# Turning the w_up blocks of a hybrid decoder layer: transposing DMA transfers of 16-bit halves in place of PE transposes

## The chip, the cores and the metric

The kernel runs on one core of one Trainium2 chip. Such a core has five engines that run side by side, each in the order of its own instruction list: TensorE (PE in the profile; it multiplies matrices and, with an identity matrix as operand, transposes), VectorE (DVE), ScalarE (ACT), GpSimd (POOL) and SyncE (SP), whose only work here is to issue DMA transfers. Sixteen DMA engines carry out the transfers of all of them. SBUF is the large on-chip memory of 128 partitions, PSUM the small one that PE writes its results to. The metric is the time of one execution in microseconds (us) on the device.

## The reference, cut to what matters

One decoder layer is computed for 256 tokens of width 2048: a mixer (a state-space half and an attention half between two projections), and then a feed-forward part of width 8192 with a squared ReLU. The change touches the feed-forward part alone:

```python
D_MODEL = 2048; SEQ = 256; DEPTH = 1; D_FF = 4 * D_MODEL

def squared_relu_mlp(u, w_up, w_down):
    hdn = jax.nn.relu(jnp.einsum('bsd,df->bsf', u, w_up))
    return jnp.einsum('bsf,fd->bsd', hdn * hdn, w_down)

def reference(...):
    ...
    h = h + rmsnorm(mix, norm_mix_post[i])
    ff = squared_relu_mlp(rmsnorm(h, norm_mlp_pre[i]), w_up[i], w_down[i])
    h = h + rmsnorm(ff, norm_mlp_post[i])
```

Everything is float32.

## The kernel before, in words

**Products in three parts.** A float32 product is made of three faster ones. Each operand x is split into a rounded part (hi, of type float32r) and the rest (lo). `split` (line 145) does it: ScalarE copies x into hi (line 147), VectorE subtracts hi from x (line 148). PE then adds hi*hi, hi*lo and lo*hi in PSUM.

**Weights.** A tile of weights is 256 rows by 512 columns, 512 KB, held as 128 partitions x 1024. SP loads it into a raw slot (line 161, `fetch`), ScalarE and VectorE split it into one of five pairs of tiles called hi and lo, and PE multiplies it with the activations. A raw slot is free again when VectorE has made lo of it, a hi/lo pair when PE has used it. `RAWS = 4` raw slots always exist; each stage adds some in buffers that lie idle (`room["raw"]`).

**Units.** The work of the projections is done in units of two column blocks (2 x 512) and 256 tokens (two token tiles t of 128), with the 2048 rows of w_up in 8 steps k. A step is done either plainly (`row_tiles`: two weight tiles, 12 matmuls each) or, for a pair of column blocks together, by a scheme of seven products in place of eight (`seven`: two loaded tiles a and b, a sum e and a half tile t4 made from them by VectorE, 21 matmuls in all). For w_up the steps 1, 3, 4 and 6 are done by `seven`. After the last of them `combine_new` puts sums of the extra accumulators into four tiles of 128x512, `room["shared"]` (made of the buffers hb and wpost), and step 7 ends the unit. The seven products need sums of the activations too (`sums_of_acts`), kept in `room["sums"]`.

**Order.** The two halves of w_up and w_down (4096 columns and rows each) are done in turn: w_up half 0 (first block otherwise, then three units), w_down half 0 (two units), w_up half 1 (four units), w_down half 1 (two units). Weight loads and splits are pushed ahead of other work (`AHEAD`); the framework's scheduler lays down the order of each engine's list, and each engine follows it in order.

**Turning.** The result of a w_up unit, 128 tokens x 512 features for each of two blocks and two token tiles, is relu'd and squared and must then be turned, features to partitions, to serve as the activations of w_down. At the end of a block `up_end` makes r on VectorE (line 1450), ScalarE applies ReLU and Square (lines 1451, 1452), and `turned` lets PE do four transposes of 128x128 (line 1463) into the PSUM bank that the block has left; `split` then writes the parts into the activation tiles (sh/sl, ah0/al0, ah1/al1). A queue `waiting` with `pump` spreads this over the following steps. There are 12 results to turn in half 0 and 16 in half 1.

**Buffers.** In half 0 the four extra raw slots of the w_up units lie in mw0, mw1 and mw2; in half 1 three extra slots lie in a buffer ha. When w_down half 0 begins, `beside_down` makes a new ha, which holds the first sums of the activations. When w_down half 1 begins, a new ha gives three of its extra raw slots, uc two others.

Of the kernel before, what the change touches and what calls it, by code (L numbers as in the profile page):

```python
# [10 lines left out]
F32 = mybir.dt.float32  # L11
F32R = mybir.dt.float32r
BF16 = mybir.dt.bfloat16
AF = mybir.ActivationFunctionType
ALU = mybir.AluOpType
# [62 lines left out]
def hymba_layer(ctx: ExitStack, tc: tile.TileContext, x, norm_mix_pre, w_in, conv_w, conv_b, dt_bias, a_log,  # L78
# [113 lines left out]
    def beside_up(raws, turn):  # L192

        room["sums"] = [v[:, k:k + KB] for k in range(0, NK // 2, KB) for v in att[1]]
        b = hp.tile([P, NT, NB], F32, name="hb")
        room["shared"] = [[b[:, t] for t in range(NT)],
                          [hp.tile([P, NB], F32, name="wpost", bufs=2) for _ in range(NT)]]
        room["raw"], room["turn"], room["acts"], room["chain"] = raws, turn, act_u, True
        sums_of.clear()
# [124 lines left out]

    def row_tile(dst, t, parts, k0, acts, begin, end, cs=slice(0, NB)):
# [9 lines left out]
    def row_tiles(src, c0, ks, acc, acts, first=True, last=True, lag=0, at_end=None, pumps=1, fetch=fetch, halves=None):  # L335
# [4 lines left out]
        for i in range(n + lag):  # L340
# [14 lines left out]
            pump(pumps)  # L355

# [94 lines left out]
    def unit(src, n, order, last, acc, more, combine, lag=0, at_end=(None, None), first=True, ending=None,  # L451
# [5 lines left out]
        for i, (k, by_seven) in enumerate(order):  # L457
            if i + 1 < len(order) and order[i + 1][1]:
                sums_of_acts(order[i + 1][0])
            if by_seven:  # L460
# [4 lines left out]
                seven(src, *cols, k, acc, more, k == sevens[0], k == sevens[-1])  # L465
            else:
# [3 lines left out]
            if k == sevens[-1]:  # L470
                combine(more)
# [973 lines left out]
    def up_end(fb, b):  # L1445

        def at_end(t, acc):
            with tc.high_priority(offset=AHEAD):
                r = tmp() if t else hp.tile([P, NB], F32, name="junk")
                nc.vector.tensor_tensor(r, acc, room["shared"][b][t], op=ALU.subtract if b else ALU.add)  # L1450
                nc.scalar.activation(r, r, AF.Relu, scale=rmlp[:, t:t + 1])
                nc.scalar.activation(r, r, AF.Square)
            waiting.append(turned(t, 4 * fb, r, acc, 1 - b))
        return at_end

    def turned(t, k, r, p, later):
        for _ in range(later):
            yield
        ts = slice(t * P, (t + 1) * P)
        with tc.high_priority(offset=AHEAD):  # L1460
            with tc.issue_after(product[0].ins), tc.issue_after(product[1].ins):
                for f in range(4):
                    nc.tensor.transpose(p[:, f * P:(f + 1) * P], r[:, f * P:(f + 1) * P], ident)  # L1463
            d_h, d_l, i = part(k)
            split(d_h[:, i:i + 4, ts], d_l[:, i:i + 4, ts], p.rearrange("p (f s) -> p f s", f=4))
# [17 lines left out]
    for hf in range(2):  # L1483
        if hf:
            a = hp.tile([P, 3 * KB, NB], F32, name="ha")
            beside_up([*(a[:, k:k + KB] for k in range(0, 3 * KB, KB))], 0)
        for fb in range(0 if hf else 2, 8, 2):
            unit(w_ups[hf], fb, orders[("up", hf), fb], (7,), acc, more,
                 lambda x: combine_new(room["shared"], x), 0, (up_end(fb, 0), up_end(fb + 1, 1)))
            acc, more = more, acc  # L1490
        if hf == 0:
# [65 lines left out]
```

## Time and profile before

| what | value |
|---|---|
| runs timed | 1453.19, 1455.0, 1452.5 us; median 1453.19 us |
| span of the profiled execution, first to last instruction | 1451.4 us |
| median of the runs less that span | 1.8 us |
| packets of DMA, bytes, mean rate | 172359, 332.97 MB, 229 GB/s |
| time of the two w_down stages and the w_up stages together | about 790 to 1437 us of the span |

The profile is of one execution. Busy time counts the stretches in which an engine had an instruction under way; instructions of one engine overlap at their ends, so that the time from start to start is less than the duration of one. A "chain" follows the work that ended last back to the start; a "releaser" is what ended an engine's idle time.

### The profile page before, as it was taken

Reading aid. Unit: us, or ns where it says so; the run is one execution under the profiler, and the core shown is the slowest. Engines: PE = TensorE matmul, PEld = TensorE weight load, DVE = VectorE, ACT = ScalarE, POOL = GpSimd, SP = SyncE. Lnnn points to the kernel's source line nnn. Section 1 sums busy time; section 2 is a strip of 40 time slices with the busy share of each in tenths; the row PEclk is TensorE's granted clock in tenths of the full one; section 3 lists DMA queues with packets and bytes.
Section 4 is the critical chain, followed back from the end, with each engine's and each line's share of the span. In section 5 each row is a group of like instructions: output and inputs, shape, how many; then the busy total and the mean of one; then the engine's idle time right before and its main releaser. Section 6 shows DMA issues by size and latency. Waiting matters only on the chain.

```text
span 1451.4 us, 20394 instructions
## 1 busy us (share of the span) xinstructions
PE 1442.4 (99%) x7042; PEld 1214.7 (84%) x7042; DVE 1300.4 (90%) x1881; ACT 947.1 (65%) x1351; POOL 162.3 (11%) x244
## 2 busy tenths in 40 slices
PE   9999999999999999999999999999999999999998
PEld 8888888888888888888888888888888888888886
DVE  7788888988999788689988999999889999999998
ACT  7577669665666666556657677656465776766664
POOL 0201110131111000010100011010111110101000
PEclk9999999999999999999999999999999999999999
DMA  8977656756898658588976798688888888788854
GB/s 267 272 219 222 189 175 187 239 170 195 231 253 248 196 127 244 173 270 257 280 225 217 210 311 240 203 221 251 249 255 279 255 245 247 210 293 265 248 179 160
DMA packets 172359, 332.97 MB, mean 229 GB/s; under 512 B 16048, under 2 KB 18976, under 8 KB 172256
## 3 DMA queue, kind: packets, MB, share of 16 engines
q1 hardware_dynamic: 144736, 272.37, 58.1%
q0 software_dynamic: 19648, 45.63, 15.7%
q10 hardware_dynamic: 7872, 13.68, 2.8%
q8 instruction: 55, 0.90, 0.3%
q14 instruction: 48, 0.39, 0.1%
HBM read 327.39 MB, written 49.84 MB: 260 GB/s over the span
## 4 chain that ended last, share of the span: by engine, by line
PE 76%; ACT 1%; DVE 1%; DMA 0%; issue 0%; ACTq 0%
PE acc L331 10%; PE acc L333 10%; PE acc L332 10%; PE acc L418 7%; PE acc L419 7%; PE acc L420 7%; PE acc L485 4%; PE ps L331 3%; PE ps L332 3%; PE ps L333 3%; PE ps L418 2%; PE ps L419 2%; PE ps L420 2%; PE acc L488 2%; PE acc L1463 1%; PE ps L938 0%
## 5 line engine op out<-in xcount | busy, mean ns | idle before, releaser
L148 DVE TENSOR_TENSOR lo<-raw,hi 128x1024 fp32r<-128x1024 f32 (+1 forms) x387 | 470.1, 1220 | 79.1 <-ACT hi L147 76.3
L147 ACT ACTIVATE hi<-raw 128x1024 fp32r<-128x1024 f32 (+1 forms) x387 | 404.2, 1050 | 204.2 <-PE acc L333 71.4
L485 PE MATMUL acc<-ua,hi 128*128 128x512 f32 x520 | 141.2, 401 | 0.1
L147 ACT ACTIVATE hi<-e 128x1024 fp32r<-128x1024 f32 x66 | 70.2, 1063 | 68.5 <-DVE e L252 62.7
L485 PEld LDWEIGHTS acc<-ua,hi 128*128 128x128 f32 x520 | 91.3, 189 | 14.2 <-ACT hi L147 0.2
L331 PE MATMUL acc<-hi,ua 128*128 128x512 f32 x228 | 90.6, 397 | 0.0
L332 PE MATMUL acc<-lo,ua 128*128 128x512 f32 x228 | 89.3, 392 | 0.0
L333 PE MATMUL acc<-hi,ua 128*128 128x512 f32 x228 | 89.2, 391 | 0.0
L331 PE MATMUL acc<-hi,sh 128*128 128x512 f32 x220 | 86.9, 395 | 0.0
L333 PE MATMUL acc<-hi,sl 128*128 128x512 f32 x220 | 85.8, 390 | 0.0
L332 PE MATMUL acc<-lo,sh 128*128 128x512 f32 x220 | 85.7, 390 | 0.0
L488 PEld LDWEIGHTS acc<-ua,lo 128*128 128x128 f32 x520 | 76.5, 190 | 8.9
L148 DVE TENSOR_TENSOR lo<-e,hi 128x1024 fp32r<-128x1024 f32 x66 | 80.5, 1220 | 0.0
L488 PE MATMUL acc<-ua,lo 128*128 128x256 f32 x520 | 78.8, 282 | 0.0
L419 PE MATMUL acc<-lo,ah 128*128 128x512 f32 x180 | 70.1, 390 | 0.0
L420 PE MATMUL acc<-hi,al 128*128 128x512 f32 x180 | 70.1, 390 | 0.0
L418 PE MATMUL acc<-hi,ah 128*128 128x512 f32 x180 | 70.1, 390 | 0.0
L485 PE MATMUL acc<-uc,hi 128*128 128x512 f32 x208 | 61.4, 405 | 0.0
L148 DVE TENSOR_TENSOR lo<-ha,hi 128x1024 fp32r<-128x1024 f32 x43 | 52.5, 1221 | 6.0 <-ACT hi L147 5.8
L147 ACT ACTIVATE hi<-ha 128x1024 fp32r<-128x1024 f32 x43 | 45.2, 1057 | 19.4 <-PE acc L333 12.4
L147 ACT ACTIVATE hi<-r 128x512 fp32r<-128x512 f32 x66 | 41.5, 629 | 20.8 <-PE acc L333 8.8
L418 PE MATMUL acc<-hi,ua 128*128 128x512 f32 x137 | 53.7, 392 | 0.0
(572 smaller groups left out, 3722.3 us busy)
## 6 DMA issues: line engine op xcount, KB each, us to landing
raw<-in_w_in_dram SPq DMA_DIRECT2D x154, 512.0 KB, 4.5
raw<-in_w_down_dram SPq DMA_DIRECT2D x69, 512.0 KB, 5.7
raw<-in_w_up_dram SPq DMA_DIRECT2D x65, 512.0 KB, 4.8
raw<-in_w_out_dram SPq DMA_DIRECT2D x38, 512.0 KB, 5.1
raw<-pair SPq DMA_DIRECT2D x57, 256.0 KB, 4.3
pair<-in_w_up_dram POOLq DMA_DIRECT2D x56, 256.0 KB, 5.4
pair<-in_w_down_dram POOLq DMA_DIRECT2D x52, 256.0 KB, 6.3
pair<-in_w_in_dram POOLq DMA_DIRECT2D x42, 256.0 KB, 5.5
```

The lines of the kernel that those rows point to most:

```text
L147: return (nc.scalar.activation(hi, src, AF.Copy), nc.vector.tensor_tensor(lo, src, hi.bitcast(F32), op=ALU.subtract))
L148: nc.vector.tensor_tensor(lo, src, hi.bitcast(F32), op=ALU.subtract))
L331: nc.tensor.matmul(dst[:, cs], a_h[:, r, ts], hi[:, j, cs], start=begin and j == 0, stop=False)
L332: nc.tensor.matmul(dst[:, cs], a_h[:, r, ts], lo[:, j, cs], start=False, stop=False)
L333: product[t] = nc.tensor.matmul(dst[:, cs], a_l[:, r, ts], hi[:, j, cs], start=False, stop=end and j == KB - 1)
L418: nc.tensor.matmul(dst, a_h, hi[:, j], start=own and first, stop=False)
L419: nc.tensor.matmul(dst, a_h, lo[:, j], start=False, stop=False)
L420: nc.tensor.matmul(dst, a_l, hi[:, j], start=False, stop=own and last)
L485: nc.tensor.matmul(acc[f], hi[:, j, f * P:(f + 1) * P], u(k0 + j), start=k0 + j == 0, stop=False, skip_group_check=True)
L488: nc.tensor.matmul(acc[f][:, 0], lo[:, j, f * P:(f + 1) * P], u(k0 + j)[:, 0], start=False, stop=k0 + j == NK - 1, skip_group_check=True)
L1463: nc.tensor.transpose(p[:, f * P:(f + 1) * P], r[:, f * P:(f + 1) * P], ident)
```

## The change

Each result r is now made in place in the tile of `room["shared"]` that held its combined sum, and is turned without PE. ScalarE takes r (32-bit words) apart: it copies the low and the high 16-bit halves into a buffer `halves`, each half on its own stretch (128x1024 of 16 bits). SP issues a transposing DMA transfer of the halves back onto r's own tile, 256 KB, in eight blocks of 128x128. ScalarE puts the 16-bit pieces together again into `halves`, read as float32, and `split` makes the two parts from there. A second queue, `beside`, is pumped once per weight tile and twice per seven-step; each of the four results of a unit takes three pumps, and `drain_beside` finishes what is left before `combine` writes the shared tiles again and at the end of a half.

Space: the buffer ha now exists in both halves of the w_up stage. Two thirds of it are the four `halves` tiles, the last third one extra raw slot. So half 0 has five extra raw slots (four before) and half 1 has one (three before).

```diff
--- before.py
+++ after.py
@@ -11,6 +11,7 @@
 F32 = mybir.dt.float32
 F32R = mybir.dt.float32r
 BF16 = mybir.dt.bfloat16
+U16 = mybir.dt.uint16
 AF = mybir.ActivationFunctionType
 ALU = mybir.AluOpType
 
@@ -195,7 +196,9 @@
         b = hp.tile([P, NT, NB], F32, name="hb")
         room["shared"] = [[b[:, t] for t in range(NT)],
                           [hp.tile([P, NB], F32, name="wpost", bufs=2) for _ in range(NT)]]
-        room["raw"], room["turn"], room["acts"], room["chain"] = raws, turn, act_u, True
+        a = hp.tile([P, 3 * KB, NB], F32, name="ha")
+        room["halves"] = [a[:, i].bitcast(U16) for i in range(2 * NT)]
+        room["raw"], room["turn"], room["acts"], room["chain"] = [*raws, a[:, 2 * NT:]], turn, act_u, True
         sums_of.clear()
 
     def beside_down():
@@ -321,6 +324,19 @@
     def drain():
         while waiting:
             pump()
+
+    beside = deque()
+
+    def pump_beside(n=1):
+        for _ in range(n):
+            if beside:
+                work = beside.popleft()
+                if next(work, work) is not work:
+                    beside.append(work)
+
+    def drain_beside():
+        while beside:
+            pump_beside()
 
     def row_tile(dst, t, parts, k0, acts, begin, end, cs=slice(0, NB)):
 
@@ -353,6 +369,7 @@
                 if at == n - 1 and at_end:
                     at_end(t, acc[t])
             pump(pumps)
+            pump_beside()
 
     def gemm_tokens(src, c0, acts, nk, lag=0, at_end=None, pumps=1):
 
@@ -463,11 +480,13 @@
                     if ready:
                         ready()
                 seven(src, *cols, k, acc, more, k == sevens[0], k == sevens[-1])
+                pump_beside(2)
             else:
                 for b in range(2):
                     row_tiles(src, cols[b], [k], acc[b::2], room["acts"], first and i == 0, False,
                               fetch=fetch_next)
             if k == sevens[-1]:
+                drain_beside()
                 combine(more)
         for b in range(2):
             if b and ending:
@@ -1446,23 +1465,23 @@
 
         def at_end(t, acc):
             with tc.high_priority(offset=AHEAD):
-                r = tmp() if t else hp.tile([P, NB], F32, name="junk")
-                nc.vector.tensor_tensor(r, acc, room["shared"][b][t], op=ALU.subtract if b else ALU.add)
+                r = room["shared"][b][t]
+                nc.vector.tensor_tensor(r, acc, r, op=ALU.subtract if b else ALU.add)
                 nc.scalar.activation(r, r, AF.Relu, scale=rmlp[:, t:t + 1])
-                nc.scalar.activation(r, r, AF.Square)
-            waiting.append(turned(t, 4 * fb, r, acc, 1 - b))
+            beside.append(turned(t, 4 * fb, r, room["halves"][NT * b + t]))
         return at_end
 
-    def turned(t, k, r, p, later):
-        for _ in range(later):
+    def turned(t, k, r, halves):
+        ts = slice(t * P, (t + 1) * P)
+        words = r.bitcast(U16)
+        nc.scalar.activation(r, r, AF.Square)
+        nc.scalar.activation(halves.rearrange("p (h n) -> p h n", h=2), words.rearrange("p (n h) -> p h n", h=2), AF.Copy)
+        nc.sync.dma_start_transpose(words.rearrange("p (n s) -> p n s", s=P), halves)
+        for _ in range(2):
             yield
-        ts = slice(t * P, (t + 1) * P)
-        with tc.high_priority(offset=AHEAD):
-            with tc.issue_after(product[0].ins), tc.issue_after(product[1].ins):
-                for f in range(4):
-                    nc.tensor.transpose(p[:, f * P:(f + 1) * P], r[:, f * P:(f + 1) * P], ident)
-            d_h, d_l, i = part(k)
-            split(d_h[:, i:i + 4, ts], d_l[:, i:i + 4, ts], p.rearrange("p (f s) -> p f s", f=4))
+        nc.scalar.activation(halves.rearrange("p (n h) -> p h n", h=2), words.rearrange("p (h n) -> p h n", h=2), AF.Copy)
+        d_h, d_l, i = part(k)
+        split(d_h[:, i:i + 4, ts], d_l[:, i:i + 4, ts], halves.bitcast(F32).rearrange("p (f s) -> p f s", f=4))
 
     def onto_new_mw(more):
 
@@ -1482,12 +1501,12 @@
     acc, more = [bank() for _ in range(2 * NT)], [psmall(), bank(), psmall(), bank()]
     for hf in range(2):
         if hf:
-            a = hp.tile([P, 3 * KB, NB], F32, name="ha")
-            beside_up([*(a[:, k:k + KB] for k in range(0, 3 * KB, KB))], 0)
+            beside_up([], 0)
         for fb in range(0 if hf else 2, 8, 2):
             unit(w_ups[hf], fb, orders[("up", hf), fb], (7,), acc, more,
                  lambda x: combine_new(room["shared"], x), 0, (up_end(fb, 0), up_end(fb + 1, 1)))
             acc, more = more, acc
+        drain_beside()
         if hf == 0:
             beside_down()
             unit(w_down, 0, orders[("down", 0), 0], (14, 15), acc, more,
```

How the change moves the work on the engines, at the two places where a w_up half is followed by w_down. Names are tiles with their numbers; hi_ and lo_ are the two parts of a weight tile. Line numbers of the changed program are its own: there line 148 is ScalarE's half of `split`, 149 VectorE's, 435 to 437 the matmuls of `seven`, 347 to 349 those of a plain step, 1478 the copy into halves, 1479 the transposing transfer, 1482 the copy back.

ScalarE at the start of w_down half 0, before: ha_9130 is the buffer of the sums (made from r_9232), ah1 the parts of the turned results, hi_9285, hi_9290, hi_9294 and hi_9298 the tiles a, e, b and t4 of the first seven-step.

```order
L147 ACTIVATE hi_9285<-raw_9274 128x1024
L147 ACTIVATE ah1_3798<-acc_8009 128x4x128
L147 ACTIVATE ha_9130<-r_9232 128x512
L147 ACTIVATE ah1_3798<-acc_8011 128x4x128
L147 ACTIVATE hi_9290<-e_9281 128x1024
L147 ACTIVATE hi_9294<-raw_9278 128x1024
L147 ACTIVATE ah1_3798<-acc_8010 128x4x128
L147 ACTIVATE hi_9298<-r_9282 128x512
```

ScalarE at the same place of the changed program: ha_7892 is the buffer with the halves, ha_9131 the one of the sums, hi_9310 and hi_9327 the two tiles of the plain step after the first seven-step (whose four tiles hi_9262, hi_9267, hi_9271 and hi_9275 lie earlier), hi_9354, hi_9359 and hi_9363 the tiles a, e and b of the second seven-step.

```order
L1482 ACTIVATE ha_7892<-wpost_7890 128x2x512
L1482 ACTIVATE ha_7892<-wpost_7891 128x2x512
L148 ACTIVATE hi_9310<-raw_9308 128x1024
L148 ACTIVATE hi_9327<-mw2_6211 128x1024
L148 ACTIVATE hi_9354<-raw_9343 128x1024
L148 ACTIVATE ah1_3798<-ha_7892 128x4x128 x2
L148 ACTIVATE hi_9359<-e_9350 128x1024
L148 ACTIVATE hi_9363<-raw_9347 128x1024
L148 ACTIVATE ha_9131<-r_9209 128x512
```

The sums now stand behind all four copies back and behind the parts of three tiles of the second seven-step, because their buffer takes the place of the one with the halves.

VectorE at this place of the changed program; its row on ha_9131 follows the last reading of ha_7892 (al1), which follows lo_9364. Before, the sum ha_9130 stood between the two sums of e of the first seven-step.

```order
L149 TENSOR_TENSOR lo_9360<-e_9350,hi_9359 128x1024
L394 TENSOR_TENSOR r_9392<-ah0_4884,al0_4885 128x512
L149 TENSOR_TENSOR lo_9364<-raw_9347,hi_9363 128x1024
L149 TENSOR_TENSOR al1_3799<-ha_7892,ah1_3798 128x4x128
L149 TENSOR_TENSOR ha_9131<-r_9209,ha_9131 128x512
```

PE at the first seven-step of w_down half 0, before: the tile a (hi_9285) and then at once the tile e (hi_9290) with the sums.

```order
L418 MATMUL ps_8012<-hi_9285,sh_79 128x512
L419 MATMUL ps_8012<-lo_9286,sh_79 128x512
L420 MATMUL ps_8012<-hi_9285,sl_80 128x512
L418 MATMUL acc_8009<-hi_9290,ha_9130 128x512
L419 MATMUL acc_8009<-lo_9291,ha_9130 128x512
L420 MATMUL acc_8009<-hi_9290,ha_9130 128x512
```

And in the changed program: the products of tile e (hi_9267) with the sums stand behind those of tile a of the second seven-step (hi_9354).

```order
L435 MATMUL ps_8013<-hi_9354,sh_79 128x512
L436 MATMUL acc_8009<-lo_9355,sh_79 128x512
L437 MATMUL acc_8009<-hi_9354,sl_80 128x512
L436 MATMUL ps_8013<-lo_9355,sh_79 128x512
L437 MATMUL ps_8013<-hi_9354,sl_80 128x512
L435 MATMUL acc_8010<-hi_9267,ha_9131 128x512
L436 MATMUL acc_8010<-lo_9268,ha_9131 128x512
L437 MATMUL acc_8010<-hi_9267,ha_9131 128x512
```

The first seven-step is cut in two, and a plain step and a part of the second seven-step have moved in between.

SP at the start of w_down half 1, before: ha_12080 is the new buffer with three raw slots, and its loads follow those into uc.

```order
L156 DMA raw_12230<-pair4_93 128x512
L157 DMA raw_12230<-in_w_down_dram 128x512
L161 DMA uc_12079<-in_w_down_dram 128x2x512 x2
L161 DMA ha_12080<-in_w_down_dram 128x2x512
L156 DMA ha_12080<-pair0_89 128x512
L157 DMA ha_12080<-in_w_down_dram 128x512
```

And in the changed program, where the new buffer is ha_12064 and the one with the halves ha_10528:

```order
L157 DMA raw_12190<-pair4_93 128x512
L158 DMA raw_12190<-in_w_down_dram 128x512
L162 DMA uc_12063<-in_w_down_dram 128x2x512 x2
L1479 DMA_TRANSPOSE hb_10525<-ha_10528 128x8x128 x2
L1479 DMA_TRANSPOSE wpost_10526<-ha_10528 128x8x128
L1479 DMA_TRANSPOSE wpost_10527<-ha_10528 128x8x128
L162 DMA ha_12064<-in_w_down_dram 128x2x512
L157 DMA ha_12064<-pair0_89 128x512
L158 DMA ha_12064<-in_w_down_dram 128x512
```

The four transposing transfers have moved in ahead of the loads into ha, and the first of these loads takes the bytes that held the halves.

## The prediction

> **What bounds the kernel now.** I read the busy times first, then the chain of work that ended last, then windows cut out of that chain.
>
> ```profile
> PE 1442.4 (99%) x7042; PEld 1214.7 (84%) x7042; DVE 1300.4 (90%) x1881; ACT 947.1 (65%) x1351; POOL 162.3 (11%) x244
> ```
>
> PE is busy 99% of the span, so work taken off PE shortens the kernel unless an engine that feeds PE becomes late. Rows of the chain in order of time (start, us, operation):
>
> ```profile
> 1150.54 0.44 PE ps L1463 x4
> 1193.20 0.44 PE acc L1463 x4
> ...
> 1278.57 0.44 PE acc L1463 x4
> ```
>
> The transposes are on the chain, and units follow each other at 42.7 us. A window for two of them, and two shorter stretches used below (start:end, length; busy us of PE, PEld, DVE, ACT, POOL with counts; granted clock of PE; share of the DMA engines; GB/s):
>
> ```profile
> 1156.90:1199.58 42.68, 42.68 (x198) 35.47 (x197) 40.30 (x50) 30.41 (x38) 5.42 (x8) 1.00 0.83 243
> 1199.60:1242.28 42.68, 42.68 (x197) 35.45 (x197) 40.30 (x50) 30.41 (x38) 5.42 (x8) 1.00 0.85 246
> 835.43:856.80 21.37, 21.37 (x96) 17.72 (x95) 19.65 (x25) 14.58 (x18) 4.07 (x6) 1.00 1.02 344
> 1028.30:1049.70 21.40, 21.40 (x96) 17.74 (x95) 16.94 (x19) 11.66 (x12) 2.74 (x5) 1.00 0.82 227
> ```
>
> In a unit PE never stops and its clock is 1.00. ACT has 12 us free, DVE little over 2. Who leads whom stands in the waits from 1150 to 1285 (waiter, releaser; us in all, times, longest):
>
> ```profile
> ACT hi L147 <- PE acc L333: 14.4, 9, 2.1
> DVE lo L148 <- ACT hi L147: 5.7, 6, 1.7
> ```
>
> ACT waits until PE gives a hi/lo pair back: the feeders run ahead of PE as far as five pairs allow.
>
> **What goes.** PE's timeline around one group of four transposes (start, us):
>
> ```profile
> 855.15 0.39 PE L332 MATMUL ps<-lo,ua 128*128 128x512 f32 x1
> ...
> 856.73 0.39 PE L333 MATMUL ps<-hi,ua 128*128 128x512 f32 x1
> 856.97 0.60 PE L1463 MATMUL acc<-ident,junk 128*128 128x128 f32 x4
> 857.32 0.48 PE L331 MATMUL acc<-hi,ua 128*128 128x512 f32 x1
> 857.63 0.40 PE L332 MATMUL acc<-lo,ua 128*128 128x512 f32 x1
> ```
>
> From 855.15 to 856.73 PE takes seven steps of 0.226 us. From 856.73 to 857.63 it takes two steps and the group: 0.90 − 2 × 0.23 = 0.44 us, as the chain has it. All transposes of the line, in its four forms:
>
> ```profile
> L1463 PE MATMUL acc<-ident,junk x44: 270/272/329, 857.0 to 1282.5; 128*128 128x128 f32 x44
> L1463 PE MATMUL acc<-ident,r x44: 270/272/273, 860.2 to 1288.4; 128*128 128x128 f32 x44
> L1463 PE MATMUL ps<-ident,junk x12: 270/272/273, 899.7 to 1236.0; 128*128 128x128 f32 x12
> L1463 PE MATMUL ps<-ident,r x12: 271/272/273, 903.0 to 1240.1; 128*128 128x128 f32 x12
> ```
>
> These are 112, or 28 groups, and 28 × 0.44 = **12.3 us** leave PE. A unit's PE time becomes 42.68 − 4 × 0.44 = 40.92 us.
>
> **What ACT gets.** Two copies of 128x1024 16-bit elements for each result. No 16-bit read and no strided write of this size is in the trace. The nearest rows are the 128x1024 copy, and two of 128x512 of which one writes 16 bits (busy us, mean ns, idle before):
>
> ```profile
> 860.54 1.05 ACT L147 ACTIVATE hi<-mw 128x1024 fp32r<-128x1024 f32 x1
> 861.49 0.58 ACT L147 ACTIVATE sh<-acc 128x512 fp32r<-128x512 f32 x1
> L575 ACT ACTIVATE junk<-xs 128x512 bf16<-128x512 f32 x8 | 5.0, 629 | 0.0
> L147 ACT ACTIVATE ha<-r 128x512 fp32r<-128x512 f32 x4 | 2.5, 632 | 1.6 <-DVE r L380 1.3
> ```
>
> A 16-bit write costs what a 32-bit one does (629 and 632 ns), so I go by elements: 1.05 us each, 0.95 from start to start (860.54 to 861.49). Below, they could take half, if 16-bit data went at double pace; above, twice, if a strided half-word cost two. I take 0.95, the nearest row. A unit then holds 30.4 + 8 × 0.95 = 38.0 us of ACT in 40.92: it fits. DVE's list keeps its instructions, 40.3 us in 40.92. It fits too, barely, and since overlapped ends count as busy there is about 1 us more room than that shows. The split reads SBUF where it read PSUM; 0 is taken, since `split`'s subtractions from the one and from the other have 687 and 686 ns:
>
> ```profile
> L148 DVE TENSOR_TENSOR lo<-r,hi 128x512 fp32r<-128x512 f32 x66 | 45.3, 687 | 0.7 <-ACT hi L147 0.7
> L148 DVE TENSOR_TENSOR al<-ps,ah 128x512 fp32r<-128x512 f32 x12 | 8.1, 686 | 1.1 <-ACT ah L147 1.1
> ```
>
> With less lead here and there, I put **0.5 us** on the units together (0 to 3).
>
> **What the queues get.** 28 transfers of 256 KB on SP. The trace has none that transposes. The nearest: copies between SBUF and DRAM of that size, and SP's queue as a whole (KB each, us to landing; packets, MB, share of 16 engines):
>
> ```profile
> h_d<-ha ACTq DMA_DIRECT2D x6, 256.0 KB, 2.3
> raw<-pair SPq DMA_DIRECT2D x57, 256.0 KB, 4.3
> ha<-h_d ACTq DMA_DIRECT2D x6, 256.0 KB, 6.7
> q1 hardware_dynamic: 144736, 272.37, 58.1%
> ```
>
> The queue moved 272.37 MB in 0.581 × 1451.4 = 843 us of all engines, 323 GB/s; 256 KB are 0.81 us by that. By packets it is 16 × 843 us / 144736 = 93 ns each; 1024 packets of 256 bytes, should the transposition cut it so, would take 1024 × 93 ns / 16 = 5.95 us. I take about 1 us of the engines and a landing of 4.3 us (bounds 2.3 and 6.7 and, with 5.95 of packets, 10). The copies back stand 6 to 11 us behind the copies into halves, so 4.3 is covered; from 6 on, ACT stops at a copy back, with the next weight's hi behind it and PE behind that. A slower transfer is also queued ahead of the weight loads.
>
> The Trainium skill (VectorE: DVE Perf Modes, "The three transpose paths") gives 390 ns for a 128x128 16-bit transpose on TensorE and 1309 ns by DMA, and its rules choose TensorE if a result in PSUM is acceptable, which speaks against this change; the trace has 0.11 us of PE for each and nothing for the DMA's side. By 1309 ns for each of eight blocks, one after the other, a transfer would take 10.5 us. The Trainium skill's page DMA: Bandwidth & Descriptors ("Latency and other measured facts") has 261 GB/s for such transfers, by which one would be an estimated 1.0 us. By the first figure the time would be that of the third rival below, by the second the sum stands; the trace so far shows neither.
>
> The raw slots, 9 for 8 in half 0 and 5 for 7 in half 1, cost nothing in my sum: in the stretch from 1028.30 (quoted above), which has five, PE lost nothing. Cover is gone where a load stands behind two transfers; its room there is about 5 us.
>
> **Stall A, at w_down half 0.** Before, the first sums ha came early, in a buffer of their own. Now that buffer takes the place of the halves, and (the rows on ACT, DVE and PE above) PE's products of hi_9267 with the sums stand right behind those of hi_9354. The sum needs, one after the other: hi_9363, which waits for the pair that PE gives back at the end of hi_9354 (ACT 1.05), lo_9364 (DVE 1.13 from start to start), al1 as the last reader of the halves (DVE 0.6), the two halves of the split into ha_9131 (ACT 0.63, DVE 0.69). The DVE steps by their rows:
>
> ```profile
> 855.65 1.22 DVE L148 TENSOR_TENSOR lo<-raw,hi 128x1024 fp32r<-128x1024 f32 x1
> 856.78 0.69 DVE L252 TENSOR_TENSOR r<-e,raw 128x512 f32<-128x512 f32 x1
> ```
>
> 1.05 + 1.13 + 0.6 + 0.63 + 0.69 = 4.1 us in which PE has nothing to do, since its list is in order. With 0.6 us for the waits between the steps and a shorter one before hi_9354, I put **+4.7 us** (3.5 to 6). It doesn't depend on how fast the transfers are.
>
> **Stall B, at w_down half 1.** SP's first load into the new ha waits for the last al1. Before, it was issued at the end of the last unit, 1278 or so:
>
> ```profile
> 1280.66 0.78 SPq L161 DMA_DIRECT2D ha<-in_w_down_dram  x1
> ha<-in_w_down_dram SPq DMA_DIRECT2D x11, 512.0 KB, 5.8
> ha<-in_w_down_dram SPq DMA_DIRECT2D x5, 256.0 KB, 4.9
> ```
>
> Now, from the last matmul of the last unit on: PE does six tiles of 12 steps and the first six steps of a seven-step, 78 × 0.227 = 17.7 us, and then gives back the pair for which hi_12261 waits on ACT. Behind this stand ah1, the last copy back, ah1 and al1: 1.05 + 0.6 + 0.95 + 0.63 + 0.69 = 3.9, so the loads are issued at about 21.8. They land 4 to 5.8 later, at 26 to 27.5; e takes two sums and a hi more, 2 × 0.6 + 1.06, so e's first product comes at about 29.5. PE would be there after 15 more steps, a plain step of 24 and two: 119 × 0.227 = 27.0. **+2.5 us** (1 to 4).
>
> **Sum.** Span 1451.4 − 12.3 + 0.5 + 4.7 + 2.5 = 1446.8. The median of the runs was 1.8 us over the profiled span, which makes 1448.6 us.
>
> **Rivals.** (1) *Full gain.* PE finds other products at the two stalls, or the pairs come free earlier than I put them: 1453.2 − 12.3 = 1440.9. For it: the lists differ from those before only at these places. Against: PE's order is fixed and the sums have one buffer. (2) *Late landings.* Transfers land at 6.7 us or more, ACT stops at some copies back, and loads wait behind them; 0.6 us in each of the seven units make 1448.6 + 4.2, about 1453. For it: the DMA engines are already at 0.83. (3) *Slower, by the DMA engines.* The transposing transfers occupy the sixteen engines for longer than the weights leave free. A unit's loads take 0.84 × 42.68 = 35.9 us of the engines, or 243 × 42.68 / 344 = 30.2 at the pace of the stretch from 835.43. Of 40.92 remain 5.0 to 10.7, so it decides from 1.25 to 2.7 us for each of four transfers. At 5.95 it costs 30.2 + 23.8 − 40.92 = 13 us in each unit, at the higher load 19: 92 to 131 us, about 1540 to 1580. For it: small packets; against: the whole queue's pace. By the Trainium skill's 1309 ns (VectorE: DVE Perf Modes) it would decide so, by its 261 GB/s not. (4) *Slower, by ACT.* The 16-bit copies take twice: 30.4 + 8 × 1.9 = 45.6 us in a unit of 40.92, 7 × 4.7 = 33 us, about 1480. Against it: the 629 ns above. (5) *The change doesn't do what it says*, with PE still transposing: excluded by the order, which has no row of it left.
>
> **How the numbers follow.** About 0.2% (2.9 us) is what a measurement of this kernel can tell from no change. Forecast 0.46, rival 1 0.12, rival 2 0.20, rival 3 0.13, rival 4 0.09. Rivals 3 and 4 make up 0.22 and are left out but for their mildest part, so the range goes from 1440.5 (rival 1) to 1468, between rival 2 and the two slow ones, where landings at 10 us would lie. Faster is all below 1450.3: 0.33 of the forecast's 0.46, rival 1, and 0.03 of rival 2, 0.48. Same is the forecast's rest and 0.11 of rival 2, 0.24. Slower is 0.06 of rival 2 and rivals 3 and 4, 0.28.
>
> **What would show it.** The profile after should have no transposes of w_up results on PE, 40.9 us from unit to unit, 56 new ACT copies of about 1.05 us, and PE idle at two places, released by DVE's sum ha at the first and by ACT's e behind a load into ha at the second. Rival 2 shows as ACT idle in front of line 1482, released by DMA; rival 3 as DMA shares near 1 in all units with landings far over 10 us; rival 4 as copies of 2 us. The prediction is wrong if PE stops inside the units, or if the two stalls are not there.

## The result, and the profile after

The changed kernel takes 1469.33 us (median of 4 runs, 1468.63 to 1470.33) where the kernel before takes 1453.16 (4 runs beside them, 1452.5 to 1455.0): a ratio of 1.0111, 95% interval 1.0096 to 1.0125. It is 16.2 us slower. The span of the profiled execution is 1468.1 us, 16.7 more than before.

The first two views of the page after, busy time and the clock of PE in 40 slices:

```profile
PE 1441.2 (98%) x6930; PEld 1209.3 (82%) x6930; DVE 1299.2 (88%) x1881; ACT 1000.9 (68%) x1407; POOL 162.4 (11%) x244
PEclk9999999999999999999999999989999999989999
```

The 112 transposes are gone from PE (7042 − 6930). Two slices show a lower clock, which no slice did before. Windows of the kernel after (columns as before): a unit of w_up, then two stretches of 30 us:

```profile
1157.14:1198.12 40.98, 40.98 (x183) 33.95 (x182) 40.19 (x49) 37.76 (x46) 5.42 (x8) 1.00 1.01 283
950.00:980.00 30.00, 19.94 (x68) 14.56 (x67) 19.57 (x29) 18.44 (x22) 2.71 (x4) 0.77 0.83 188
1300.00:1330.00 30.00, 21.35 (x69) 15.40 (x68) 19.62 (x27) 18.20 (x23) 1.90 (x3) 0.77 0.81 255
```

In the unit PE never stops: 40.98 us for what took 42.68. The loss is in two stretches, where each half of w_up hands over to w_down. There PE does 68 and 69 matmuls in 30 us, and in the unit 134 in as long (183 in 40.98), so it loses 66 × 0.227 = 15.0 us at the first place and 65 × 0.227 = 14.8 at the second. With the 12.3 us that went: 29.8 − 12.3 = 17.5, about the 16.7 of the spans.

**The first place.** ACT's timeline (in brackets: idle before, and what ended it), and PE's waits with a few steps behind them:

```profile
942.50 1.04 ACT L1478 ACTIVATE ha<-hb 128x1024 uint16<-128x1024 uint16 x1
...
949.23 1.04 ACT L1478 ACTIVATE ha<-wpost 128x1024 uint16<-128x1024 uint16 x1
950.17 1.04 ACT L148 ACTIVATE hi<-raw 128x1024 fp32r<-128x1024 f32 x1
952.95 1.35 ACT L1482 ACTIVATE ha<-hb 128x1024 uint16<-128x1024 uint16 x1 [1.73 <-DMA hb<-ha]
955.31 1.34 ACT L1482 ACTIVATE ha<-hb 128x1024 uint16<-128x1024 uint16 x1 [1.01 <-DMA hb<-ha]
956.52 0.60 ACT L148 ACTIVATE hi<-r 128x512 fp32r<-128x512 f32 x1
957.03 1.13 ACT L148 ACTIVATE ah<-ha 128x512 fp32r<-128x512 f32 x2
958.17 2.54 ACT L1482 ACTIVATE ha<-wpost 128x1024 uint16<-128x1024 uint16 x2
960.58 1.03 ACT L148 ACTIVATE hi<-raw 128x1024 fp32r<-128x1024 f32 x1
```

```profile
957.18 0.79 PE L435 MATMUL ps<-hi,sh 128*128 128x512 f32 x1 [3.74 <-ACT hi L148]
...
961.66 1.22 PE L347 MATMUL ps<-hi,sh 128*128 128x512 f32 x2 [2.54 <-ACT hi L148]
...
963.63 0.63 PE L349 MATMUL ps<-hi,sl 128*128 128x512 f32 x1
964.06 0.63 PE L347 MATMUL ps<-hi,sh 128*128 128x512 f32 x1
...
973.09 0.80 PE L435 MATMUL acc<-hi,ha 128*128 128x512 f32 x1 [3.78 <-ACT ha L148]
```

Inside a unit the copies back (L1482) find their data there. Here all four come in a burst, the first of them one hi behind the last copy into halves (L1478). ACT waits for the first two transfers, and the hi of the next tiles stand behind the copies back. PE waits for hi at 957.18 (t4) and at 961.66 (the plain step), and at 973.09 for the sum. After each stop PE steps at 0.43 us (963.63 to 964.06) for some microseconds.

**The second place**, on ACT, on SP and on PE:

```profile
1285.68 1.04 ACT L1478 ACTIVATE ha<-hb 128x1024 uint16<-128x1024 uint16 x1
...
1298.64 2.56 ACT L1482 ACTIVATE ha<-hb 128x1024 uint16<-128x1024 uint16 x2 [3.32 <-DMA hb<-ha]
1314.76 1.06 ACT L148 ACTIVATE hi<-ha 128x1024 fp32r<-128x1024 f32 x1 [6.01 <-DMA ha<-in_w_down_dram]
```

```profile
1286.74 8.69 SPq L1479 DMA_TRANSPOSE hb<-ha  x2
1295.53 4.07 SPq L1479 DMA_TRANSPOSE wpost<-ha  x2
1309.50 0.37 SPq L162 DMA_DIRECT2D ha<-in_w_down_dram  x1
```

```profile
1301.72 0.51 PE L435 MATMUL ps<-hi,sh 128*128 128x512 f32 x1 [1.31 <-ACT hi L148]
1305.42 0.80 PE L347 MATMUL ps<-hi,sh 128*128 128x512 f32 x1 [2.23 <-ACT hi L148]
...
1307.70 0.63 PE L347 MATMUL ps<-hi,sh 128*128 128x512 f32 x1
1308.12 0.63 PE L348 MATMUL ps<-lo,sh 128*128 128x512 f32 x1
...
1315.87 0.50 PE L435 MATMUL acc<-hi,sh 128*128 128x512 f32 x1 [1.90 <-ACT hi L148]
1319.12 0.80 PE L435 MATMUL acc<-hi,ua 128*128 128x512 f32 x1 [2.52 <-ACT hi L148]
```

First ACT waits for a transfer, then for the weights whose raw slot in ha was free only after the last reading of the halves. PE stops twice behind the burst of copies back and twice behind the loads into ha.

### The profile page after: what moved, and what is told of

The parts are those of the page before. It is cut to its first block, busy times and chain, and to the rows that moved or that the text cites. A ratio compares the mean times of both kernels' runs of the same rounds, so it can differ in the third digit from the quotient of the medians.

```text
span 1468.1 us, 20247 instructions
## 1 busy us (share of the span) xinstructions
PE 1441.2 (98%) x6930; PEld 1209.3 (82%) x6930; DVE 1299.2 (88%) x1881; ACT 1000.9 (68%) x1407; POOL 162.4 (11%) x244
## 4 chain that ended last, share of the span: by engine, by line
PE 69%; DMA 3%; ACT 3%; DVE 2%; issue 1%; SPq 0%; ACTq 0%; DVEq 0%
PE acc L347 9%; PE acc L349 9%; PE acc L348 9%; PE acc L435 6%; PE acc L436 6%; PE acc L437 6%; PE acc L504 4%; PE ps L347 3%; PE ps L348 3%; PE ps L349 3%; PE ps L437 2%; PE ps L436 2%; PE ps L435 2%; PE acc L507 2%; DMA hb<-ha 1%; DMA raw<-in_w_down_dram 1%
## 5 line engine op out<-in xcount | busy, mean ns | idle before, releaser
L149 DVE TENSOR_TENSOR lo<-raw,hi 128x1024 fp32r<-128x1024 f32 (+1 forms) x402 | 486.8, 1217 | 82.1 <-ACT hi L148 80.2
L148 ACT ACTIVATE hi<-raw 128x1024 fp32r<-128x1024 f32 (+1 forms) x402 | 419.4, 1049 | 199.2 <-PE acc L349 62.2
L347 PE MATMUL acc<-hi,ua 128*128 128x512 f32 x228 | 90.1, 395 | 0.0
L348 PE MATMUL acc<-lo,ua 128*128 128x512 f32 x228 | 89.3, 391 | 0.0
L349 PE MATMUL acc<-hi,ua 128*128 128x512 f32 x228 | 89.1, 391 | 0.0
L435 PE MATMUL acc<-hi,ua 128*128 128x512 f32 x137 | 53.3, 399 | 2.5 <-ACT hi L148 2.5
L436 PE MATMUL acc<-lo,ua 128*128 128x512 f32 x137 | 53.7, 392 | 0.0
L437 PE MATMUL acc<-hi,ua 128*128 128x512 f32 x137 | 53.6, 391 | 0.0
L149 DVE TENSOR_TENSOR lo<-r,hi 128x512 fp32r<-128x512 f32 x66 | 45.2, 684 | 7.9 <-ACT hi L148 7.6
```

What stands on the lines that cost most here:

```text
L148: return (nc.scalar.activation(hi, src, AF.Copy), nc.vector.tensor_tensor(lo, src, hi.bitcast(F32), op=ALU.subtract))
L149: nc.vector.tensor_tensor(lo, src, hi.bitcast(F32), op=ALU.subtract))
L347: nc.tensor.matmul(dst[:, cs], a_h[:, r, ts], hi[:, j, cs], start=begin and j == 0, stop=False)
L348: nc.tensor.matmul(dst[:, cs], a_h[:, r, ts], lo[:, j, cs], start=False, stop=False)
L349: product[t] = nc.tensor.matmul(dst[:, cs], a_l[:, r, ts], hi[:, j, cs], start=False, stop=end and j == KB - 1)
L435: nc.tensor.matmul(dst, a_h, hi[:, j], start=own and first, stop=False)
```

## The experiments

The time before was 1452.9 to 1453.2 us beside each group of runs. "Lost steps" is the excess of PE's steps in the profile of a run, from start to start, over 0.227 us (15.1 and 14.6 us at the two places of the changed kernel).

**Where the loss is: `pe_last` and `pe_last_h1`.** The units at the ends are turned by PE again, with the code of before (`turned_pe`); in `pe_last_h1` only in half 1 (`hf and fb == 6`).

```diff
         for fb in range(0 if hf else 2, 8, 2):
+            end = up_end_pe if fb == 6 else up_end
             unit(w_ups[hf], fb, orders[("up", hf), fb], (7,), acc, more,
-                 lambda x: combine_new(room["shared"], x), 0, (up_end(fb, 0), up_end(fb + 1, 1)))
+                 lambda x: combine_new(room["shared"], x), 0, (end(fb, 0), end(fb + 1, 1)))
```

> The last unit of each half is turned by PE, as before; the other five units keep the transposing transfers. Theory (transitions): all of the loss lies at the two places where a half of w_up is followed by w_down, 15.1 us of lost PE steps at the first and 14.6 at the second, and the units inside do save 0.44 us for each group. Then 1469.3 - 29.7 + 8 x 0.44 = 1443 us, and PE stands nowhere between the units. Rival (everywhere): the transposing transfers and the slow copies back hold up each unit; with five of seven units still so, 1453.2 + 16.1 x 5 / 7 = 1465 us.

> Only the last unit of half 1 is turned by PE. Transitions theory: the first place keeps its loss of 15.1 us, the second loses its 14.6: 1469.3 - 14.6 + 4 x 0.44 = 1456.5 us. Rival (the second place's loss follows from the first, since the loads run late from there on): the second place is already whole while the first stays, about 1453 to 1455, or, if losses are spread over all units, 1467 us.

Measured: `pe_last` 1454.05 us, ratio 1.0011 (1.0002 to 1.0020); `pe_last_h1` 1464.57, 1.0082 (1.0066 to 1.0098). The place is right: without transfers at the ends 15 us of the 16 are gone. But 11 us are missing to 1443, and at the ends PE now waits for something else. PE and ACT of `pe_last` (L1492 is PE's transpose there, L1481 the Square):

```profile
942.86 0.66 PE L1492 MATMUL acc<-ident,junk 128*128 128x128 f32 x4 [2.62 <-ACT junk L1481]
```

```profile
940.00 1.06 ACT L148 ACTIVATE hi<-raw 128x1024 fp32r<-128x1024 f32 x1 [2.60 <-DMA raw<-in_w_down_dram]
```

The Square of r stands behind a hi that waits for its weights: the first loads of w_down are late. `pe_last_h1` came to neither figure, 8 us above the theory and 2 below the rival's 1467. The second place loses 4.0 us instead of 14.6, while the first stays and even grows to about 21 in the profiled run, which was the slowest of the four (1469.40 us): ACT waits 6.2 us for transfers there, in the changed kernel 2.7.

**Whether the transfer itself is slow: `plain`.**

```diff
-        nc.sync.dma_start_transpose(words.rearrange("p (n s) -> p n s", s=P), halves)
+        nc.sync.dma_start(words, halves)
```

> The transposing transfers are plain transfers of the same 256 KB, so that the results are not turned (the output is another); lists and waits stay. Theory (the transposing transfer itself is slow: to issue, 1.2 to 5.3 us of SP, and to land): the copies back no longer wait at the two places, the first two PE waits of each go, and the time falls to about 1457 us; the third wait at the first place (for the sums, 3.8 us) and the wait for the loads into ha (about 4.7 us) stay. Rival (the place in the list alone: a copy back so close behind its copy into halves waits for any transfer): 1466 us or more.

Measured: 1466.63 us (1.0097, 1.0082 to 1.0113), as the rival has it. ACT of `plain` at the first place:

```profile
951.14 2.56 ACT L1482 ACTIVATE ha<-hb 128x1024 uint16<-128x1024 uint16 x2 [0.82 <-DMA hb<-ha]
953.57 0.60 ACT L148 ACTIVATE hi<-r 128x512 fp32r<-128x512 f32 x1
954.08 1.14 ACT L148 ACTIVATE ah<-ha 128x512 fp32r<-128x512 f32 x2
955.63 2.53 ACT L1482 ACTIVATE ha<-wpost 128x1024 uint16<-128x1024 uint16 x2 [0.41 <-DMA wpost<-ha]
958.03 1.03 ACT L148 ACTIVATE hi<-raw 128x1024 fp32r<-128x1024 f32 x1
```

Even a plain transfer is waited for here, and with hardly a wait the four copies back, two splits and a half tile's hi keep ACT from the next weight tile from 951.1 to 958.0. ACT's waits at the copies back are 1.2 us in all, where the changed kernel has 6.1, and yet PE loses 13.4 and 12.0 us at the two places in the profiled run (15.1 and 14.6 in the changed kernel). Being a transposition costs 2.7 us of the 16 (1469.3 − 1466.6; the four runs of `plain` go from 1464.2 to 1469.3), its long issue on SP included.

**The buffer of the sums: `sums_first`.**

```diff
-        room["sums"] += [m[:, t].rearrange("p (b s) -> p b s", b=2) for t in range(NT)]
+        room["sums"] = [m[:, t].rearrange("p (b s) -> p b s", b=2) for t in range(NT)] + room["sums"]
```

> At the start of w_down half 0 the first sums go into the buffer m, which is free, and the later ones into ha: the sums no longer wait for the last reading of the halves. Theory (the third wait at the first place is for the buffer): the 3.8 us wait for ha goes, with some 1.5 us of slow steps behind it: about 1464 us; the first two waits there, which are for copies back, stay. Rival (PE would wait there for the split tiles behind the same copies back anyway): 1468 to 1469 us.

Measured: 1462.70 us (1.0063, 1.0041 to 1.0085). The time is near the theory's 1464. In the profiled run, the fastest of the four (1458.2 to 1466.5 us), the wait for ha fell from 3.8 to 0.7 us and the first place from 15.1 to 6.6 us of lost steps:

```profile
955.95 0.50 PE L435 MATMUL ps<-hi,sh 128*128 128x512 f32 x1 [0.27 <-ACT hi L148]
959.14 0.49 PE L347 MATMUL ps<-hi,sh 128*128 128x512 f32 x1 [1.73 <-ACT hi L148]
970.00 0.50 PE L435 MATMUL acc<-hi,ha 128*128 128x512 f32 x1 [0.69 <-ACT ha L148]
```

The buffer was a cause of its own, and not through the third wait alone: the first two waits, which the theory left as they were, shrank as well (3.74 to 0.27 and 2.54 to 1.73). With its sums at hand PE does the twelve products of tile e before t4, and these 2.7 us cover a part of ACT's burst; ACT itself waits for the first two transfers as before (1.23 and 0.90 us).

**The raw slots: `before_slots`, `slots8`, `pe_last_slots`, `mix`.** The late loads of `pe_last` led to the count of raw slots. Slots are used in turn; w_down begins again with the four that always exist. In half 0 with nine slots, and in half 1 with five, the last four tiles of w_up lie in just these.

```diff
-        room["raw"], room["turn"], room["acts"], room["chain"] = [*raws, a[:, 2 * NT:]], turn, act_u, True
+        room["raw"], room["turn"], room["acts"], room["chain"] = [*raws, *([] if raws else [a[:, 2 * NT:]])], turn, act_u, True
...
-            beside_up([], 0)
+            beside_up([], -RAWS)
```

`slots8` has the first edit; `pe_last_slots` both and that of `pe_last`; `mix` both and that of `sums_first`; `before_slots` is the kernel before with the slots of the change.

> The kernel before, all turned by PE, with the raw slots of the change: nine in half 0 of w_up, five in half 1. With nine slots the last four tiles of half 0 lie in the four slots that the first loads of w_down take, with eight they don't; with five it is so in half 1. Theory (slots): that makes the first loads of w_down late, and what ACT holds behind their copies; the run with PE in the last units fell short of 1443 us by 11 us for this reason, so here some 8 to 11 us are lost too, most of them at the ends of the halves: 1461 to 1464 us. Rival (SP's queue): the loads are late because transposing transfers stand ahead of them; there are none here: 1453 to 1454 us.

> The changed kernel, with the eight raw slots of before in half 0 of w_up (the last third of ha lies idle there); half 1 as changed. Slots theory: the first four loads of w_down half 0 are issued some 6 us earlier than in the changed kernel (923.9 there), ACT no longer waits for them, r, halves, transfers and copies back all come earlier, and of the first two waits of PE at the first place (3.9 and 2.7 us and the slow steps behind them) most goes: about 1461 us. Rival (a copy back waits for its transfer wherever it stands): 1467 us or more.

> PE turns the last unit of each half, half 0 has the eight slots of before, and in half 1 the count of the five slots begins four earlier, so that the last tile of w_up lies in ha and the first load of w_down has a slot that is free for longer. Slots theory: the losses that remained with PE in the last units (5.4 us at the first place, 1.8 within half 1, 4.0 at the second) go at the first place and shrink at the second: 1444 to 1448 us. Rival (SP's queue): 1452 us or more.

> The changed kernel with three repairs and all transfers kept: eight slots in half 0, the five slots of half 1 counted from four earlier, and the first sums of w_down half 0 in the buffer m. Slots theory: the gains add up, 1469.3 - 8 (loads) - 6.6 (sums, as measured) - 2 to 3 (half 1): about 1452 us, with most of the second place's loss still there (its loads into ha wait for the halves). Rival (copies back set the time at both places): 1460 us or more.

Measured: `before_slots` 1457.65 us (1.0032, 1.0019 to 1.0044), half of the loss that was expected; `pe_last_slots` 1450.10 (0.9980, 0.9971 to 0.9989), 4 us below `pe_last` and between theory and rival; `slots8` 1468.31 (1.0110, 1.0097 to 1.0124), as the rival has it; `mix` 1459.54 (1.0044, 1.0031 to 1.0058), far from the theory's 1452 and next to the rival's 1460. So the slots alone cost 4.7 us where PE turns, and in half 0 nothing clear of the noise where the transfers stand at the end. `slots8` shows why. SP's rows of the changed kernel, then SP's and ACT's of `slots8`:

```profile
923.91 6.07 SPq L162 DMA_DIRECT2D raw<-in_w_down_dram  x4
...
946.19 5.69 SPq L1479 DMA_TRANSPOSE hb<-ha  x2
```

```profile
915.65 6.44 SPq L162 DMA_DIRECT2D raw<-in_w_down_dram  x4
...
943.69 8.08 SPq L1479 DMA_TRANSPOSE hb<-ha  x2
```

```profile
952.84 1.36 ACT L1482 ACTIVATE ha<-hb 128x1024 uint16<-128x1024 uint16 x1 [4.71 <-DMA hb<-ha]
```

The loads begin at 915.65, in the changed kernel at 923.91, and the first transfer is issued at 943.69 for 946.19. Yet its copy back starts at 952.84, as before at 952.95: the transfer took 9.2 us instead of 6.8, and ACT only waits longer.

**Repairing the order: `fix`, `fix_h0`, `fix_order`, `fix2`.** All transfers stay. `fix` and `fix_h0` have the slots of `mix` too, `fix_order` those of the changed kernel. At the ends the copies back are tied behind the weight tiles of the step after the first seven-step, and the new ha is taken after them, by `more_sums` in half 0 and `more_slots` in half 1:

```diff
+        with ExitStack() as order:
+            if "tied" in room:
+                order.enter_context(tc.issue_after(line["act"].ins))
+            nc.scalar.activation(halves.rearrange("p (n h) -> p h n", h=2), words.rearrange("p (h n) -> p h n", h=2), AF.Copy)
...
+    def more_sums():
+        drain_beside()
+        del room["tied"]
+        a = hp.tile([P, 3 * KB, 2, S], F32R, name="ha")
+        b = hp.tile([P, KB, 2, S], F32R, name="hb")
+        room["sums"] += [b[:, k] for k in range(KB)] + [a[:, k] for k in range(3 * KB)]
```

> The changed kernel with all its transfers, but at both ends of the halves the four copies back are tied behind the weight tiles of the plain step that follows the first seven-step of w_down; the sums go first into m and hb, the new ha is taken only after the copies back, its raw slots in half 1 only from the 13th load on; eight slots in half 0, and the five of half 1 counted from four earlier. Theory (order at the transitions): PE stands nowhere for over 1 us, the clock stays at 1.00, and the 12.3 us are whole: 1441 to 1446 us. Rival (the transfers land too late there wherever the copies stand, since they share the DMA engines with the loads; 9 us in the run with eight slots): ACT waits at the copies back all the same and PE with it, 1450 us or more.

> The same repair at the first transition only; at the second the copies back stand as in the changed kernel. Theory: the first place is whole, the second keeps its loss of about 10.6 us (as with the three repairs of the run mix), so about 11 us over the repair of both: 1453 to 1456 us. Rival (the second place's loss comes from late loads of half 1, not from its copies back): as far below as the repair of both, within 3 us of it.

> The repair of the order and of the buffers at both transitions, with the raw slots of the changed kernel (nine in half 0, five in half 1, counted as there). Slots theory, second form: late first loads of w_down cost time as soon as nothing later hides them, 3 to 5 us (with PE in the last units it was 4.0): 1446 to 1449 us. Rival (slots matter only for PE's own transposes, which wait for r at once; copies back tied so far behind give the loads time): within 1.5 us of the run with all repairs.

Measured: `fix` 1453.91 us (1.0011, 1.0002 to 1.0020); `fix_h0` 1462.63 (1.0065, 1.0051 to 1.0079); `fix_order` 1456.89 (1.0025, 1.0015 to 1.0035). The repair is worth 15 us, its part at the second place 8.7 of them, and the slots, which are in it, 3.0. None came to its number, and `fix` lies where its rival put it; the differences between the three came nearer to the theories (8.7 for about 11, 3.0 for 3 to 5). PE of `fix` at the first place, and ACT and SP at the second (L443 is a matmul of `seven` there, L1493 the transfer, L1501 the copy back):

```profile
985.14 0.80 PE L443 MATMUL acc<-hi,ha 128*128 128x512 f32 x1 [3.67 <-ACT ha L148]
```

```profile
1297.63 1.37 ACT L1501 ACTIVATE ha<-hb 128x1024 uint16<-128x1024 uint16 x1 [3.23 <-DMA hb<-ha]
```

```profile
1287.88 3.38 SPq L162 DMA_DIRECT2D raw<-in_w_down_dram  x2
1291.31 5.15 SPq L1493 DMA_TRANSPOSE hb<-ha  x2
```

The wait for a sum in ha has moved to the third seven-step, because the last al1 (983.75) stood behind the lo of eight weight tiles and a half one on DVE; and the transfers, of whose halves the first were ready at 1281.4, stood in SP's list behind loads that waited, so that ACT still stopped at a copy back. `fix2` pushes the parts of the last results ahead, and in half 1 the copies into halves with their transfers:

```diff
+        soon = tc.high_priority(offset=AHEAD) if room.get("last") else ExitStack()
+        with soon:
+            nc.scalar.activation(r, r, AF.Square)
...
+            nc.sync.dma_start_transpose(words.rearrange("p (n s) -> p n s", s=P), halves)
...
+        with tc.high_priority(offset=AHEAD) if tied else ExitStack():
+            d_h, d_l, i = part(k)
+            split(d_h[:, i:i + 4, ts], d_l[:, i:i + 4, ts], halves.bitcast(F32).rearrange("p (f s) -> p f s", f=4))
```

> The run fix with two more changes of order: the parts (ah1, al1) of the four last results of each half are pushed ahead like weights, so that the last reading of the halves at the first place no longer stands behind five weight tiles on VectorE (the wait for the third sum in ha, 3.7 us); and in half 1 the four copies into halves and their transfers are pushed ahead, so that the transfers no longer stand in SP's list behind loads that wait for a raw slot (in fix the first was ready at about 1281.4 and issued at 1291.3). Theory (lists: each remaining wait is an instruction queued behind something slower): the first place's 7.1 us fall to 1 or 2, the second's 6.1 to about 3, 1445 to 1448 us. Rival (the feeders are short at the second place whatever the order, with six raw slots and the burst of ACT work): the second place stays at 6, 1449 to 1452 us.

Measured: 1451.27 us (0.9988, 0.9976 to 1.0000), in the rival's range. In the profiled run (1449.25 us) the first place lost 0.7 us, with one wait of 0.44 left. The second place still lost 4.5 us, and half 1 lost 4.4 more about a unit ahead of it, in short waits and slow steps.

**Half 0 alone: `half0`**, which is `fix2` in half 0, and in half 1 the kernel before, with seven raw slots.

```diff
+            end = up_end_pe if hf else up_end
```

> Half 0 of w_up as in fix2 (transposing transfers, the order repaired at its end); half 1 as in the kernel before: PE turns, seven raw slots. Theory: half 0 keeps its full gain of 12 x 0.44 = 5.3 us less the 0.7 us that fix2 still lost at the first place, and half 1 costs what it cost before: 1453.0 - 5.3 + 0.7 = 1448.4 us. What fix2 still lost (about 9 us) then belongs to half 1, to its transfers with five raw slots. Rival (the transfers of half 0 leave the feeders short well into w_down, or the time is lost elsewhere): 1451 us or more.

Measured: 1448.12 us (0.9968, 0.9956 to 0.9980), as the theory has it. In the profiled run (1449.33 us) the first place lost 1.5 us and the second nothing. It beats both kernels, by 4.9 and 21 us.

## Why the prediction was wrong

It forecast 1448.6 us, faster, and a range to 1468; it is 1469.3. At the two ends 4.7 + 2.5 = 7.2 us of loss were forecast, and 29.8 came.

**The gain was right.** A unit takes 40.98 us (predicted 40.92), with 37.76 us of ACT in it (38.0). In the units PE lost 0.6 us, for which 0.5 stood. `half0` came out with 0.44 us for each of its 12 groups. That ACT's total fits is in part luck: the eight copies of that unit take 9.6 us (four of 1.04 and four of 1.36), where 7.6 was put, and the rest of ACT's list takes less than its 30.4.

**The step that failed is the cover of the copies back.** "The copies back stand 6 to 11 us behind the copies into halves, so 4.3 is covered; from 6 on, ACT stops", and their work was put down as spread over a unit. Inside the units that holds: a copy back starts 9.9 to 12.5 us after the end of its copy into halves, and ACT never waits there for more than 0.06 us. At a half's end there are no pumps to wait for and the queue is drained at once. ACT is at the first copy back after 7.7 us at the first place (943.54 to 951.22) and after 8.6 at the second (1286.72 to 1295.32). That is still within the 6 to 11, but the data come only after 9.4 and 11.9. At the first place 2.6 of these pass before SP issues the transfer (946.19), with loads ahead of it on its list; from issue to landing it takes 6.8 and 11.9, and 6.6 in the median of the 28, where 4.3 was taken and 10 was the upper end. This is the second rival, at the ends alone.

But `plain` says that the landing was the smaller part: with nearly all of ACT's waits at the copies back gone, 2.7 us came back. The larger part had no term in the sum: drained at once, four copies back and the parts of the results stand in front of the hi that PE needs next, and the new ha is free only behind them. `fix`, which changes both, got 15 us back, 3.0 of them by the slots. The rows of the order that the section on the change shows for ACT begin with two copies back; what stands ahead of them was not asked.

**Stall A** was right in its own step: 4.1 us of an empty PE predicted (4.7 with the reserve), 3.78 measured, independent of the transfers (3.78 in `plain` too). It was the third of three waits. The two before it, 3.74 and 2.54 us, were not in the sum.

**Stall B** had the right mechanism and the wrong time. The loads into ha were put at 21.8 us after the last matmul of the unit. The first matmul of w_down follows that one at 1279.86. So the loads, at 1309.50, came after 29.6 us, since the copies back ahead of them waited and then came in a burst. PE's two waits there were 1.90 and 2.52 us, 4.4 together against the 2.5 predicted, and two more stood ahead of them, 1.31 and 2.23 us.

**The clock was not in the sum.** The idle time in front of PE's matmuls is 10.1 us at the first place (3.74 + 2.54 + 3.78); PE lost 15.1. Most of the rest are steps of 0.43 us in place of 0.227, with a granted clock of 0.77 over the 30 us. The last stop there shows the price: from 968.92, the last matmul before it, to 976.12 PE does eight steps in 7.20 us, where 8 × 0.227 = 1.82 were due. A stop of 3.78 us cost 5.4. The Trainium skill (TensorE: Matmul & The Clock Gate, "Part 1: The HAM clock gate") has the array at half rate after an idle window of about 3.4 us, with 426.7 ns for a matmul of 512 columns; the trace agrees with 0.43 us behind a stop of 3.74. At the second place, though, the same steps follow a stop of 2.23 us (1307.70 to 1308.12), with one of 1.31 shortly before it, so here shorter stops bring them too.

**The raw slots "cost nothing in my sum"** was wrong where something waits directly on r: 4.7 us in `before_slots`. With the transfers it was 3.0 us in `fix_order`, and nothing clear in `slots8`. It was judged by a stretch of five slots in steady turn, and not by the point where the turn begins anew.

**The transfer** was put at about 1 us of the engines. Row q1 went from 58.1% of 1451.4 us and 144736 packets to this:

```profile
q1 hardware_dynamic: 174304, 279.72, 60.8%
```

That is (0.608 × 1468.1 − 0.581 × 1451.4) / 28 = 1.8 us for each, an estimate, and 1056 packets. The Trainium skill's page DMA: Bandwidth & Descriptors ("Latency and other measured facts") would have an estimated 1.0 us by its 261 GB/s, which it gives for one kernel; the estimate from this trace is 149 GB/s, and decides. The third rival needed 1.25 to 2.7 us for each; at 1.8, and with a DMA share of 1.01 in the unit, units still kept their pace.

Settled by the runs: the places, the part of the landing, of the sums' buffer and of the slots, and what the repair of order and buffers together brings. Not settled: how order and buffer share the second place, since `fix` changes both there, and what in half 1 still costs some 9 us in `fix2`. `half0` shows that it belongs to half 1's own transfers with five slots, not which of the two. That slow steps follow from idle alone was seen in each profile with long waits, and not tried by itself.

## What to carry to other kernels

A transfer in place of an engine's work is free only where other work stands between its issue and its reader, on every list that it passes. Check this at the ends of loops, where a queue is drained, and not in the middle. And when a ring of buffers changes its length, look at where its turn begins anew.

## What the hardware showed that was not expected

Issuing a transposing transfer kept SP for 1.2 to 5.3 us. A plain transfer of the same 256 KB (`plain`) kept it for 0.5 in the median, a load of 512 KB for 0.4. Here is one in a unit of the kernel after; the first two at the ends of the halves took 5.7 and 8.7 together (946.19 and 1286.74 above):

```profile
1167.34 1.24 SPq L1479 DMA_TRANSPOSE wpost<-ha  x1
```

Being plain did not make a transfer land much sooner: 5.9 us in the median of `plain`, 6.6 in the changed kernel.

And ACT's write of every second half-word is slower than its read of them, 1.36 us against 1.04 for 128x1024 elements, of 16 bits both:

```profile
L1482 ACT ACTIVATE ha<-hb 128x1024 uint16<-128x1024 uint16 x14 | 18.9, 1358 | 6.1 <-DMA hb<-ha 6.1
L1478 ACT ACTIVATE ha<-hb 128x1024 uint16<-128x1024 uint16 x14 | 14.6, 1042 | 0.0
```
